# Row halves in turn for the first mixer's scores, and a new order of operations

## The chip, the cores and the metric

The kernel runs on one core of a Trainium2 chip. Its engines are TensorE (PE, with its weight loads as PEld), VectorE (DVE), ScalarE (ACT), GpSimd (POOL) and SyncE (SP), which issues most transfers. The metric is the device time of one execution in microseconds; less is better.

## The reference

A trunk of two layers over 256 tokens of 1024 channels, in fp32. Layer 0 mixes tokens with sliding-window attention with sinks, layer 1 with latent attention, and each mixer stands between two half-step SwiGLU feed-forwards with 2816 hidden channels:

```python
for i in range(DEPTH):
    x = x + 0.5 * swiglu(rmsnorm(x, ffn_norm1[i]), ffn1_wg[i], ffn1_wu[i], ffn1_wd[i])
    h = rmsnorm(x, mix_norm[i])
    if i % N_MIXERS == 0:
        x = x + sliding_window_attention(h, positions, rel_bias, a_w_in[j], ...)
    else:
        x = x + latent_attention(h, positions, b_w_in[j], ...)
    x = x + 0.5 * swiglu(rmsnorm(x, ffn_norm2[i]), ffn2_wg[i], ffn2_wu[i], ffn2_wd[i])
```

The first mixer has 16 query heads of 64 channels and two key and value heads, each for eight query heads:

```python
scores = jnp.einsum('bnqkgd,bnskd->bnkgqs', q, kb) * scale + bias
scores = jnp.where(valid, scores, NEG)
m = jnp.maximum(jnp.max(scores, axis=-1, keepdims=True), sink)
p = jnp.exp(scores - m)
denom = jnp.sum(p, axis=-1, keepdims=True) + jnp.exp(sink - m)
o = jnp.einsum('bnkgqs,bnskd->bnqkgd', p / denom, vb)
```

The scores' contraction thus runs over 64 channels, half of PE's 128 rows.

## The kernel before

The tokens are two tiles of 128 (t = 0 and 1). Every large weight comes in pieces of 128 x 1024 (`raw`); ACT casts a piece to a rounded high part (`whi`, line 402), and DVE subtracts to get the low part (`wlo`, line 397). A product then takes three matmuls: high by high, high by low, low by high (lines 735 to 737, 783 and 854).

Feed-forward: in chunks of 256 hidden channels, gate and up (line 854), then on DVE and ACT the gate function (lines 860 to 870), in which the product `h` is cast to a high part (line 656 on ACT, 660 on DVE) and a low part is subtracted (870), then down (783).

First mixer (`mixer_a`): per token tile, keys and values (KV), the queries in two halves of eight heads, norms, and transposes (line 688) of keys to `kTa` and of queries to `q`. In `q`, two heads lie above one another, the even one in partitions 0 to 63, the odd one in 64 to 127. Then for each key head g and parity par: the scores of four heads (line 1063), softmax (`softmax4`), transposes of p (688) and a copy to `pT`. When both parities are done, one operation multiplies by the values (line 1089, "PV"): the even heads write partitions 0 to 63 of the accumulator and the odd ones 64 to 127. The output projection (735 to 737, into `acc`) follows. For t = 0 four heads' scores of 128 columns fill one PSUM bank, for t = 1 (256 columns) two banks.

`softmax4` reads the scores with their bias out of PSUM on DVE (line 896, head by head, with the maximum), has exps and their sums on ACT (920), sums and reciprocal on DVE, and scales p in two portions (941 on DVE, 943 on ACT, 945 on POOL). PSUM has four banks named `w` for all of this, and an operation that needs a bank waits until the last reader of an earlier one has ended.

The order isn't the order of the code. Every operation is recorded with an engine (or several to choose from), an estimated cost and what it reads and writes. `Plan.run` then plays the program through by these costs: of the operations that are ready it takes the one that could start first, corrected by a table of penalties by the operation's name and engine (`PEN`), and within a stream of PE's operations it looks `WINDOW` places ahead; `SKEW` shifts the second tile's priority against the first's. Where an operation on PE that needs a new bank would start late, by over `FILLMIN`, the planner puts filler matmuls of 128 x 128 on the identity (line 1348) into that bank. It also has an idea of PE's clock (`pe_time`). The instructions are issued in the order that results, and the chip follows it engine by engine.

Two lines set which heads share a group before: `rows = slice(par * HD, (par + 1) * HD)`, one row half for all four, and `h = 8 * g + 2 * i + par`, so every second head.

## Time and profile before

| what | value |
|---|---|
| median of 3 runs (lowest to highest) | 953.3 us (952.58 to 954.87) |
| the profiled execution | 955.77 us, span 954.0 us |
| mean granted TensorE clock | 0.994 |
| PE busy | 940.6 us, 99% |
| DVE busy | 654.8 us, 69% |
| ACT busy | 490.4 us, 51% |
| POOL busy | 49.4 us, 5% |
| DMA | 160.07 MB, mean 168 GB/s |

The span goes from the first to the last instruction, and the execution's own time is a little longer. Busy PE includes the fillers, and matmuls are pipelined: a row's duration is longer than its distance from the next start. An fp32 matmul leaves two records in the trace, so 16 score matmuls are "x32", and one filler is two records; matmuls on the rounded parts leave one.

### The profile page before, as it was taken

To read this page: it belongs to the slowest core of one execution; us is meant where nothing else is said; L and a number is where in the kernel's file an instruction comes from. 1 tells how busy PE (TensorE), PEld (TensorE's weight loads), DVE (VectorE), ACT (ScalarE), POOL (GpSimd) and SP (SyncE) were. 2 spreads that over 40 slices of the span, in tenths; PEclk is the share of its full clock that TensorE was granted. 3 is DMA by queue.
4 is the path that set the end of the run, shared out by engine and by line. 5 is a ranking of instruction groups with operands and counts; after the bars stand their busy time and mean duration, and the time that the engine had idled before them with its cause. 6 is when DMAs were issued, how large, how long until landed. Compare 5 with 4: busy or idle time off the path is not lost.

```text
span 954.0 us, 16706 instructions
## 1 busy us (share of the span) xinstructions
PE 940.6 (99%) x6378; PEld 842.6 (88%) x6378; DVE 654.8 (69%) x1283; ACT 490.4 (51%) x854; POOL 49.4 (5%) x117
## 2 busy tenths in 40 slices
PE   8999999999999999999999999999999999999998
PEld 6999999988668999999989999998868889999997
DVE  6787777786767765666686656566698677565662
ACT  7484666355556543544464434443587445344540
POOL 2000000013000000000010000000431000000000
PEclk9999999999799999999999999999999999999999
DMA  8766556545115666565655656656201477556441
GB/s 287 232 209 209 167 176 192 165 133 179 43 45 178 219 200 199 166 200 165 201 172 173 204 178 187 203 162 199 95 1 46 141 238 225 192 177 209 159 140 45
DMA packets 119632, 160.07 MB, mean 168 GB/s; under 512 B 9264, under 2 KB 102912, under 8 KB 119552
## 3 DMA queue, kind: packets, MB, share of 16 engines
q1 hardware_dynamic: 119552, 159.00, 53.2%
q8 instruction: 50, 0.82, 0.4%
q14 instruction: 30, 0.25, 0.1%
HBM read 157.92 MB, written 1.05 MB: 167 GB/s over the span
## 4 chain that ended last, share of the span: by engine, by line
PE 93%; DVE 3%; DMA 2%; ACT 1%; issue 1%; SPq 0%; POOL 0%; DVEq 0%; ACTq 0%
PE w L854 47%; PE acc L783 26%; PE w L688 3%; PE acc L735 2%; PE acc L737 2%; PE acc L736 2%; PE w L735 1%; PE w L737 1%; PE w L736 1%; DMA raw<-in_ffn_wu_dram 1%; DVE wlo L397 1%; PE w L1262 1%; PE w L1209 1%; PE w L1063 1%; PE acc L1089 1%; PE acc L1274 1%
## 5 line engine op out<-in xcount | busy, mean ns | idle before, releaser
L854 PE MATMUL w<-xs,whi 128*128 128x256 f32 x2560 | 458.3, 282 | 0.0
L854 PEld LDWEIGHTS w<-xs,whi 128*128 128x128 f32 x2560 | 395.4, 189 | 3.4 <-ACT whi L402 0.2
L397 DVE TENSOR_TENSOR wlo<-raw,whi 128x1024 fp32r<-128x1024 f32 (+2 forms) x295 | 352.4, 1215 | 53.1 <-ACT whi L402 50.0
L402 ACT CAST whi<-raw 128x1024 fp32r<-128x1024 f32 (+2 forms) x295 | 303.8, 1042 | 121.1 <-PE acc L783 68.1
L854 PE MATMUL w<-xs,wlo 128*128 128x256 f32 x1280 | 360.5, 282 | 0.8 <-DVE wlo L397 0.8
L854 PEld LDWEIGHTS w<-xs,wlo 128*128 128x128 f32 x1280 | 241.0, 188 | 1.0 <-DVE wlo L397 1.0
L862 ACT ACTIVATE th<-h 128x256 f32<-128x256 f32 x80 | 33.5, 419 | 202.6 <-DVE h L860 202.6
L783 PE MATMUL acc<-wlo,pT 128*128 128x512 f32 x352 | 113.5, 396 | 0.0
L783 PE MATMUL acc<-whi,pT 128*128 128x512 f32 x352 | 113.5, 396 | 0.0
L783 PE MATMUL acc<-whi,t 128*128 128x512 f32 x352 | 113.3, 396 | 0.0
L860 DVE TENSOR_TENSOR h<-w,rb 128x256 f32<-128x256 f32 x80 | 34.0, 424 | 112.3 <-PE w L854 111.2
L783 PEld LDWEIGHTS acc<-whi,t 128*128 128x128 f32 x352 | 66.1, 188 | 16.3
L783 PEld LDWEIGHTS acc<-wlo,pT 128*128 128x128 f32 x352 | 66.1, 188 | 15.4
L783 PEld LDWEIGHTS acc<-whi,pT 128*128 128x128 f32 x352 | 63.4, 189 | 12.0
L870 DVE TENSOR_TENSOR t<-h,pT 128x256 fp32r<-128x256 f32 x80 | 34.0, 425 | 28.4 <-ACT pT L656 27.6
L864 DVE SCALAR_TENSOR_TENSOR th<-th,w 128x256 f32<-128x256 f32 x80 | 33.5, 419 | 26.5 <-ACT th L862 26.5
L656 ACT CAST pT<-h 128x256 fp32r<-128x256 f32 x61 | 24.8, 406 | 32.2 <-DVE h L866 32.0
L735 PE MATMUL acc<-whi,xs 128*128 128x512 f32 x96 | 39.9, 415 | 0.1
L737 PE MATMUL acc<-whi,xs 128*128 128x512 f32 x96 | 38.2, 398 | 0.4 <-DVE xs L674 0.4
L736 PE MATMUL acc<-wlo,xs 128*128 128x512 f32 x96 | 37.8, 394 | 0.0
L920 ACT ACTIVATE p<-p,st 128x128 f32<-128x128 f32 (+1 forms) x64 | 31.2, 491 | 10.2 <-DVE st L911 6.6
L735 PE MATMUL w<-whi,xs 128*128 128x512 f32 (+2 forms) x96 | 36.2, 377 | 0.0
(190 smaller groups left out, 814.6 us busy)
## 6 DMA issues: line engine op xcount, KB each, us to landing
raw<-in_ffn_wd_dram SPq DMA_DIRECT2D x88, 512.0 KB, 4.7
raw<-in_ffn_wg_dram SPq DMA_DIRECT2D x175, 256.0 KB, 3.9
raw<-in_ffn_wu_dram SPq DMA_DIRECT2D x175, 256.0 KB, 4.3
raw<-in_a_w_in_dram SPq DMA_DIRECT2D x10, 512.0 KB, 4.5
raw<-in_a_w_out_dram SPq DMA_DIRECT2D x8, 512.0 KB, 4.1
raw<-in_b_w_out_dram SPq DMA_DIRECT2D x8, 512.0 KB, 3.8
raw<-in_b_w_in_dram SPq DMA_DIRECT2D x4, 416.0 KB, 3.5
whi<-in_b_w_uq_dram SPq DMA_DIRECT2D x4, 384.0 KB, 3.1
```

Of the source, the lines that this page charges most:

```text
L397: V.tensor_tensor(out=lo[:, c], in0=raw[:, c], in1=hi.t.bitcast(F32)[:, c], op=ALU.subtract)
L402: op("ACT", c_act(m), lambda c=c: A.copy(out=hi[:, c], in_=raw[:, c]), [(raw, key_)], [(hi, key_)], seq="wh", pen=pen, prio=pr, name="W")
L735: T.matmul(o, lhsT=hi, rhs=wh, start=start, stop=False)
L736: T.matmul(o, lhsT=hi, rhs=wl, start=False, stop=False)
L737: T.matmul(o, lhsT=lo, rhs=wh, start=False, stop=stop)
L783: T.matmul(acc[nh].t, lhsT=a[:, ft, t0 : t0 + P], rhs=wt[:, nh * 512 : (nh + 1) * 512], start=(c == 0 and ft == 0 and i == 0), stop=(final ...
L854: T.matmul(o, lhsT=wt[:, sl], rhs=xs[:, p, :, kt], start=(kt == j == i == 0), stop=(kt == KT - 1 and j == 1 and i == 2))
L860: op("DVE", 0.345, lambda h=h, ps=ps: V.tensor_tensor(out=h.t, in0=ps[:, :FC], in1=rb.t, op=ALU.mult), [ps, rb], [h], name=nm)
L862: op("ACT", c_act(FC, 0.05), lambda th=th, h=h: A.activation(th.t, h.t, AF.Tanh, scale=0.5), [h], [th], name=nm)
L864: op("DVE", 0.345, lambda th=th, ps=ps: V.scalar_tensor_tensor(out=th.t, in0=th.t, scalar=1.0, in1=ps[:, :FC], op0=ALU.add, op1=ALU.mult), ...
L870: op("DVE", 0.36, lambda h=h, hthi=hthi, htlo=htlo, fb=fb: V.tensor_tensor(out=htlo[:, fb], in0=h.t, in1=hthi[:, fb].bitcast(F32), op=ALU. ...
L920: A.activation(pv(i), pv(i), AF.Exp, bias=nm[:, i : i + 1], scale=1.0 if scale is None else scale[:, i : i + 1], accum_out=den[:, i : i + 1],)
```

## The change

Four consecutive heads now form a group, so that within it even and odd heads alternate, one in each row half, into one bank for the even and one for the odd. Softmax is called on these two banks; for t = 0 both are read into one tile of p. The product with the values follows each group, on half of the accumulator's columns.

```diff
@@ mixer_a
-            o, pTs = buf(f"acc{t}", [P, 512]), []
-            for par in range(2):
-                name = f"S{t}.{g}{par}"
-                rows = slice(par * HD, (par + 1) * HD)
-                banks = [buf("w", [P, 512]) for _ in range(t + 1)]
-                for k, bk in enumerate(banks):
-                    def fn(k=k, bk=bk, rows=rows, g=g):
-                        for i in range(k * per, (k + 1) * per):
-                            T.matmul(
-                                bk[:, (i % per) * nk : (i % per + 1) * nk], lhsT=qT[rows, 4 * g + i, :],
-                                rhs=kT[rows, g, :nk], start=True, stop=True,
-                            )
-
-                    pe(t, 4, 512 * C_MM, fn, [(qT, g)] + [(kT, j) for j in range(t + 1)], [bk], name)
+            o = buf(f"acc{t}", [P, 512])
+            for hf in range(2):
+                name = f"S{t}.{g}{hf}"
+                banks = [buf("w", [P, 512]) for _ in range(2)]
+
+                def fn(banks=banks, g=g, hf=hf):
+                    for i in range(2):
+                        for par in range(2):
+                            rows = slice(par * HD, (par + 1) * HD)
+                            T.matmul(banks[par][:, i * nk : (i + 1) * nk], lhsT=qT[rows, 4 * g + 2 * hf + i, :],
+                                     rhs=kT[rows, g, :nk], start=True, stop=True)
+
+                pe(t, 4, nk * 2 * C_MM, fn, [(qT, g)] + [(kT, j) for j in range(t + 1)], banks, name)
...
-            def pvf(g=g, pTs=pTs, o=o):
-
-                for kt in range(t + 1):
-                    for par in range(2):
-                        T.matmul(o[par * HD : (par + 1) * HD, :], lhsT=sha["v", kt][:, g * HD : (g + 1) * HD],
-                                 rhs=pTs[par][kt].t, start=(kt == 0), stop=(kt == t))
+                def pvf(g=g, hf=hf, pT=pT, o=o):
+
+                    for kt in range(t + 1):
+                        for par in range(2):
+                            T.matmul(o[par * HD : (par + 1) * HD, hf * 256 : (hf + 1) * 256],
+                                     lhsT=sha["v", kt][:, g * HD : (g + 1) * HD],
+                                     rhs=pT[kt][:, par * 256 : (par + 1) * 256], start=(kt == 0), stop=(kt == t))
@@ the first weight's load
-                def load(j=j):
+                def load(j=j, q=nc.sync if len(wtiles) else nc.scalar):
@@ the planner's numbers (a few of them)
-WINDOW = 20
+WINDOW = 26
-SKEW = [1, 7, 8, 3, 4, 2]
+SKEW = [1, 7, 5, 7, 8, -5]
-    "S": {"ACT": 0.1, "PE": -0.2},
+    "S": {"ACT": 0.1, "PE": -0.05, "POOL": 0.15, "*": 0.05},
-POOLPEN = 1
-FILLMIN, FILLFROM = 0.5, 2.0
+POOLPEN = 0
+FILLMIN, FILLFROM = 0.35, 2.0
```

The table of penalties has new numbers in nearly every row, some costs are new, and the planner's idea of the clock has another threshold. So the order is new in the whole program. In numbers of instructions: fillers 34 before and 26 after, namely 8 and 9 at the start, 8 and 9 in the first mixer, 18 and 8 in the second. The casts of `h` (80 in the shared chunks) were 61 on ACT and 19 on DVE and are all on DVE. Of the 64 scalings of p, POOL had none and has 12.

PE in the first mixer's attention, before: line 1063 are the scores (`kTa` by `q`; 128 columns for the first token tile, 256 for the second), 688 the transposes of keys (`kna`) and of p, 1348 the fillers, 1089 PV.

```order
L688 MATMUL w<-ident,kna 128x128 x2
L1348 MATMUL w<-ident 128x128 x3
L1063 MATMUL w<-kTa,q_2869 128x128 x16
L688 MATMUL w<-ident,kna 128x128 x2
L1348 MATMUL w<-ident 128x128 x5
L1063 MATMUL w<-kTa,q_2938 128x256 x6
L688 MATMUL w<-ident,p 128x128 x8
L1063 MATMUL w<-kTa,q_2938 128x256 x2
L1089 MATMUL acc_3170<-pT,va_96 64x512 x2
L688 MATMUL w<-ident,p 128x128 x4
```

PE in the same place after, from the third group of the first tile on; lines 1080, 697, 1103 and 1363 are what 1063, 688, 1089 and 1348 were, `t` is the queries before their transposes, and 744 and 745 are projections.

```order
L1080 MATMUL w<-kTa,q_2804 128x128 x4
L697 MATMUL w<-ident,kna 128x128 x2
L1080 MATMUL w<-kTa,q_2804 128x128 x4
L697 MATMUL w<-ident,p 128x128 x8
L1103 MATMUL acc_3101<-pT,va_96 64x256 x2
L1080 MATMUL w<-kTa,q_3001 128x256 x4
L1103 MATMUL acc_3101<-pT,va_96 64x256 x2
L697 MATMUL w<-ident,t_3118 128x128 x4
L1080 MATMUL w<-kTa,q_3001 128x256 x4
L1363 MATMUL acc_3159<-ident 128x128
L744 MATMUL acc_3159<-whi,xs 128x512
L745 MATMUL acc_3159<-wlo,xs 128x512
```

The sixteen score matmuls of the first tile stood in one row and now stand in four groups of four; the first two of them are ahead of this piece, the first with 12 projections of 256 columns behind it, the second with 24 of 512 (six of them ahead of one set of transposes). The five fillers stand eleven rows below this piece.

DVE in the same place after: 909 are the reads of scores, 920 and 923 the maximum with the sink, 946 and 947 sum and reciprocal, 406 the low part of a weight, 1044 the scaling of the second tile's keys.

```order
L406 TENSOR_TENSOR wlo<-raw,whi 128x1024
L920 SCALAR_TENSOR_TENSOR st<-st,nsink 128x4
L923 TENSOR_TENSOR st<-sink,st 128x4
L406 TENSOR_TENSOR wlo<-raw,whi 128x1024
L946 TENSOR_TENSOR st<-st 128x4
L947 RECIPROCAL st<-st 128x4
L406 TENSOR_TENSOR wlo<-raw,whi 128x1024
L946 TENSOR_TENSOR st<-st 128x4
L947 RECIPROCAL st<-st 128x4
L909 ISA p,st<-w,S_849 128x128
L909 ISA st 128x1
```

And before, at the end of the first tile's scores, with the lines 896, 906, 909, 932 and 933 for the same operations:

```order
L1030 TENSOR_SCALAR kTa<-w,ka 128x2x128
L906 SCALAR_TENSOR_TENSOR st<-st,nsink 128x4
L909 TENSOR_TENSOR st<-sink,st 128x4
L896 ISA p,st<-w,S_1336 128x128
L896 ISA st 128x1
L896 ISA p,st<-w,S_1336 128x128
L896 ISA st 128x1
```

No low part of a weight stood between these reads; now three stand ahead of the third group's. Between the first and the last read of the first mixer's scores there were three of them and are seven.

PE at the end of the second mixer's attention, before: 1260 and 1262 are its scores for the second tile, 1274 its product with the values.

```order
L1262 MATMUL w<-S_8142 128x128
L1274 MATMUL acc_8351<-pT,q_7779 64x128 x4
L1348 MATMUL w<-ident 128x128 x13
L688 MATMUL w<-ident,p 128x128 x8
L735 MATMUL acc_8455<-whi,xs 128x512
```

And after, with 1275, 1277 and 1289 for these:

```order
L1363 MATMUL w<-ident 128x128 x3
L1275 MATMUL w<-S_7860,S_8316 128x128
L1277 MATMUL w<-S_8316 128x128
L1275 MATMUL w<-S_7860,S_8316 128x128
L1277 MATMUL w<-S_8316 128x128
L1275 MATMUL w<-S_7860,S_8316 128x128
L1277 MATMUL w<-S_8316 128x128
L1275 MATMUL w<-S_7860,S_8316 128x128
L1277 MATMUL w<-S_8316 128x128
L1363 MATMUL w<-ident 128x128 x2
L697 MATMUL w<-ident,p 128x128 x8
L744 MATMUL acc_8455<-whi,xs 128x512
```

Before, sixteen score matmuls (two groups of heads) stood ahead of this piece without a break, and six projections between its transposes of p and the next ones. Now eight stand together and the group before them earlier, and 24 projections lie between the two sets of transposes.

## Rows read from the trace of the kernel before

**Rows 1.** The page: busy time of PE, and the chain's share by engine.
```profile
PE 940.6 (99%) x6378; PEld 842.6 (88%) x6378; DVE 654.8 (69%) x1283; ACT 490.4 (51%) x854; POOL 49.4 (5%) x117
...
PE 93%; DVE 3%; DMA 2%; ACT 1%; issue 1%; SPq 0%; POOL 0%; DVEq 0%; ACTq 0%
```

**Rows 2.** Stretches: from:to, length, busy us (x instructions) by engine, granted clock, DMA.
```profile
0.00:11.45 11.45, 7.64 (x36) 6.10 (x37) 5.37 (x16) 7.06 (x16) 3.89 (x20) 1.00 0.75 234
...
236.60:249.25 12.65, 10.48 (x80) 8.30 (x80) 11.52 (x73) 8.67 (x40) 0.70 (x1) 1.00 0.14 43
249.25:259.49 10.24, 10.24 (x28) 6.05 (x26) 6.67 (x29) 3.82 (x13) 0.00 (x0) 0.50 0.16 51
...
670.00:735.20 65.20, 63.13 (x419) 50.00 (x418) 53.05 (x210) 47.20 (x141) 22.72 (x40) 1.00 0.12 37
```

**Rows 3.** PE in order of time at the start: start, duration, what, [idle before].
```profile
8.91 0.50 PE L736 MATMUL w<-wlo,xs 128*128 128x512 f32 x1 [0.94 <-DVE wlo L397]
...
10.46 1.25 PE L688 MATMUL w<-ident,x 128*128 128x128 f32 x8 [0.83 <-DMA x<-in_x_dram]
```

**Rows 4.** PE in order of time, first mixer.
```profile
236.83 0.83 PE L1348 MATMUL w<-ident 128*128 128x128 f32 x6
237.69 2.88 PE L1063 MATMUL w<-kTa,q 64*128 64x128 f32 x32
...
241.04 1.38 PE L1348 MATMUL w<-ident 128*128 128x128 f32 x10
242.82 2.10 PE L1063 MATMUL w<-kTa,q 64*128 64x256 f32 x12 [0.40 <-DVE kTa L1030]
244.85 0.72 PE L688 MATMUL w<-ident,p 128*128 128x128 f32 x4
247.22 0.63 PE L688 MATMUL w<-ident,p 128*128 128x128 f32 x4 [1.64 <-DVE st L932]
...
251.42 3.77 PE L1063 MATMUL w<-kTa,q 64*128 64x256 f32 x8
...
262.63 0.60 PE L688 MATMUL w<-ident,p 128*128 128x128 f32 x4
262.99 0.48 PE L735 MATMUL acc<-whi,xs 128*128 128x512 f32 x1
...
267.25 1.13 PE L1063 MATMUL w<-kTa,q 64*128 64x256 f32 x4
268.31 0.50 PE L735 MATMUL acc<-whi,xs 128*128 128x512 f32 x1
268.64 0.39 PE L736 MATMUL acc<-wlo,xs 128*128 128x512 f32 x1
268.87 0.40 PE L737 MATMUL acc<-whi,xs 128*128 128x512 f32 x1
```

**Rows 5.** PE in order of time, end of the second mixer's attention.
```profile
731.41 3.17 PE L1348 MATMUL w<-ident 128*128 128x128 f32 x26
734.41 1.04 PE L688 MATMUL w<-ident,p 128*128 128x128 f32 x8
```

**Rows 6.** DVE's groups by form, 236.5 to 285 us: count | busy us, mean ns | idle before.
```profile
L896 DVE CUSTOM_DVE_ANT_0 p<-w,S 128x256 f32<-128x256 f32 x16 | 6.0, 415 | 0.0
L397 DVE TENSOR_TENSOR wlo<-raw,whi 128x1024 fp32r<-128x1024 f32 x4 | 4.9, 1216 | 0.0
L896 DVE CUSTOM_DVE_ANT_0 p<-w,S 128x128 f32<-128x128 f32 x16 | 3.6, 285 | 0.0
```

**Rows 7.** ACT's groups by form in the same stretch.
```profile
L920 ACT ACTIVATE p<-p,st 128x128 f32<-128x128 f32 x16 | 6.2, 387 | 2.6 <-DVE st L906 2.6
```

**Rows 8.** The feed-forward: a stretch inside it, and the casts of h over the whole span.
```profile
350.00:650.00 300.00, 300.00 (x2073) 278.22 (x2072) 195.84 (x290) 137.97 (x180) 2.71 (x10) 1.00 0.61 185
...
L656 ACT CAST pT<-h 128x256 fp32r<-128x256 f32 x61 | 24.8, 406 | 32.2 <-DVE h L866 32.0
L660 DVE CAST pT<-h 128x256 fp32r<-128x256 f32 x19 | 5.6, 295 | 0.7
```

## Prediction before the run

> **What bounds the kernel now.** I read the page's busy times and chain first [rows 1]. TensorE (PE) is busy for 940.6 of 954.0 us and holds 93% of the chain, so a gain must come out of PE's own time: fewer or faster matmuls, fewer idle stretches, or less time at the low clock. Busy doesn't mean useful, though. The planner puts filler matmuls (line 1348) where it expects PE to wait, a filler counts as busy, and so does a matmul at half clock. So I went on to the stretches [rows 2] and to PE in order of time [rows 3 to 5]. In both feed-forward pairs around the mixers PE has no gap at all at the full clock, as in 350 to 650 us [rows 8]; there is nothing to win there. What can be won lies in four places.
>
> First, the first mixer's attention, 236.6 to 268 us. The scores of all sixteen heads of the first token tile start together at 237.69, and from then on PE waits for sixteen heads of softmax: 0.83 and 1.38 us of fillers, idle times of 0.40 and 1.64 us [rows 4], while VectorE (DVE) is busy for 11.52 of 12.65 us [rows 2]. Second, right behind the 1.64 us comes a stretch of 10.24 us in which the granted clock is 0.50, the lower of the two levels (1.2 GHz) [rows 2]: 5.1 us lost. Third, the end of the second mixer's attention: 26 filler records (13 fillers) run for 3.17 us before the transposes of p at 734.41 [rows 5]. Fourth, the first 11.45 us, where PE is busy for 7.64 us and waits 0.94 us for a weight's low part and 0.83 us for x [rows 2, 3].
>
> The profiled execution took 955.77 us (span 954.0), 2.5 us over the median of 953.3. I make the sum against 955.8 and scale the result by 953.3/955.8.
>
> **Scores in both row halves.** A score matmul has 64 rows of contraction. Before, all those of one parity, thus one row half, stand in a row. Eight records of one half alone take 3.77 us at the half clock, 0.47 each, so 0.236 at the full clock [rows 4]. But the twelve records at 242.82, eight of one half and then four of the other, take 2.10 us, not 12 x 0.236 = 2.83 [rows 4]: the four of the other half have run beside the first eight. So the row halves do overlap, and the after-order, which alternates them and gives each half its own bank, can pair all records. Before, the six runs take 2.88 + 2.10 + 1.13 + 3.77/2 + 1.13 + 1.13 = 10.3 us at the full clock (the 1.13 of 267.25 is a row; the two others of its kind are like it) [rows 4]. After, four runs of 256 columns take 4 x 0.236 = 0.94 each and four of 128 columns half of that, together 5.7, and with 0.15 us of entry and tail for each of eight groups 6.9. That is -3.4 us of PE time; bounds: -4.6 (perfect pairs) and 0 (no more overlap than now).
>
> What is it worth when DVE has to read the scores out? DVE's reads take 3.6/16 = 0.23 us a head in the first tile and 6.0/16 = 0.38 in the second [rows 6], so 0.9 and 1.5 us for four heads, against 0.6 and 1.1 us in which PE will make them. PE is then ahead of its reader, where before it was about level. The Trainium skill, page "TensorEngine Tiling (Array Packing)", section "PSUM Bottleneck", says just that: tiling speeds up the matmuls and not the evacuation of PSUM, which may become the bound. By it the -3.4 would be 0. It is a rival below. I keep -3.4, because more other work stands between the scores than before: between the first and last score matmul 36 projections of 512 columns and 12 of 256, where there were 24 of 512.
>
> **Price of more runs.** The score runs grow from six to seven and those of PV from four to seven, so there are eight more passages between 64-wide and 128-wide matmuls. After a run of scores the first projection takes 0.50 instead of 0.39 us; after a run of full 128 x 128 transposes (ahead of 262.99) it takes 0.48 [rows 4]. The passage from 64 rows thus costs no more than any other, some 0.1 us. The same page, section "Key Properties", has it that changing the tiling mode drains the engine; the row shows at most 0.02 us for it. Eight passages at 0.1 would be 0.8, but half of them replace other passages: +0.4, bounds 0 and 0.8.
>
> **Order of the first mixer.** The scores of the first tile now come in four portions with projections between them, so softmax starts earlier behind other work. PE gives up there what it has now, 0.83 + 1.38 us of fillers and 0.40 + 1.64 us idle, 4.2 us. What comes instead? The order has nine fillers there (before eight); five took 1.38 us [rows 4], so nine some 2.5. Then DVE: it has 7 casts of a weight's low part between its first and last read of scores, where it had 3, each 1.22 us [rows 6]. Three of them stand before the reads that free the banks of the first tile's last group: three casts 3.7, four reads 0.9, the two reads waited for 0.5, and about ten small operations that I estimate at 1.4, make 6.5 us, against 18 projections x 0.23 us [rows 4] + transposes and scores (some 1.4) = 5.5 us on PE. So PE waits some 1.0 us there, then about as much again, in pieces, for the second tile's keys and the transposes behind them. Before the five fillers, the softmax of the third group needs four exps of 0.39 us and sums behind two casts [rows 6, 7]; I take 1.0 us beyond the fillers. Smaller waits for PV's operands 1.2. Together 6.7 us: +2.5 against now; bounds -1.7 (fillers alone) and +7.4 (all four added casts, 4.9 us, exposed as well).
>
> **The half clock.** In the trace it fell after a stretch that held a 1.64 us idle time, single-half scores and short transposes [rows 4], and nowhere else between the start and the output. The waits that I expect are shorter and lie apart, with projections between them; the scores fill both halves. I take it as gone: -5.1, with 0 as the other bound.
>
> **Second mixer.** Before, the scores of the second tile's last two groups stand together, and both softmaxes are waited for with PE empty: 13 fillers, 3.17 us [rows 5]. After, those groups stand apart, with five fillers around the last one, and 24 projections instead of 6 lie between the two sets of transposes of p. 13 fillers fewer 5 are worth 8 x 3.17/13 = 2.0 us. DVE, 53.05 of 65.2 us busy there [rows 2], also loses 12 scalings of p to ScalarE (ACT) and GpSimd. -2.0, bounds -3.2 and +1 (the waits that fillers no longer show come back as idle).
>
> **Start.** The first weight's four loads go to ACT's queue, beside those of x on SP's. The two waits of 0.94 and 0.83 us [rows 3] can shrink, but four more issues stand before ACT's table load and squares, and x now shares the transfers: -0.4, bounds -1.5 and +0.8.
>
> **Moved at no cost.** In the feed-forward all 80 casts of h go to DVE, where 61 were on ACT: 0.295 instead of 0.406 us each [rows 8]. That adds 18 us to DVE over some 700 us in which it is idle for a third (195.84 of 300 us busy [rows 8]) and PE has no gap; it also saves a change of engine in the chain. 0; if DVE were late there, PE would stop at the next chunk for one cast, 0.3 us.
>
> **Sum:** -3.4 + 0.4 + 2.5 - 5.1 - 2.0 - 0.4 = -8.0, so 947.8 for such an execution, and 945 as a median.
>
> **Rivals.** (1) The low clock comes back: DVE's casts make PE wait over 1.5 us in one piece, as at 245.6, and PE runs at 0.50 for another 10 us. For it speaks that the waits I expect are of about that size; against it, that the order puts fillers and projections between. 945 + 5.1 less some 0.5 us of waits that lie inside = 949.6. (2) DVE is the limit of the attention, and the faster scores only wait longer for their reader: 945 + 3.4 = 948.4. The 91% busy DVE of 236.6 to 249.25 [rows 2] speaks for it, the added projections against. (3) The row halves don't pair up, so the change doesn't do what it says: also 948.4. The twelve records speak against it. (4) Slower: DVE's order in the first mixer. All four added casts are exposed (4.9 us) and the low clock comes back twice (10.2 us): 945 + 15.1 = 960. It becomes slower than before once waits and low clock together give back more than 8 us, so one recurrence alone isn't enough; DVE would have to hold PE for over 3 us besides.
>
> **How the numbers follow.** Forecast 0.53 (941 to 948), (1) 0.23, (2) 0.12, (3) 0.04, (4) 0.08. A measurement of this kernel can tell about 0.3%, 2.9 us, from no change. Faster (under 950.4): nearly all of the forecast, 0.6 of (1), 0.7 of (2) and (3): 0.52 + 0.14 + 0.11 = 0.77. Slower (over 956.2): most of (4), 0.07. The rest, 0.16, within. The range reaches from the forecast's better bound, 940, to the upper part of (1), 952.
>
> **What would show it.** Right: score runs of 128 columns of about 0.6 us and of 256 columns of about 1.1 for four heads, records in pairs; no stretch at the clock 0.50 between 230 and 270 us; the filler run at the second mixer's end at 0.7 us or less. Wrong: PE idle behind the casts of line 397 for over 1.5 us in one piece, the clock at 0.50 in the first mixer, or a gap on PE in the feed-forward waiting for the cast of h.

## The result and the profile after

| | before | after |
|---|---|---|
| median (lowest to highest) | 952.94 us (952.19 to 954.87) | 939.66 us (939.45 to 942.47) |
| ratio, 95% interval | | 0.9864 [0.9841, 0.9888] |
| the profiled execution | 955.77 us, span 954.0 | 939.52 us, span 937.7 |
| mean granted clock | 0.994 | 1.0 |

Faster by 13.3 us, more than forecast and 0.3 us beyond the better end of the range. Of the changed kernel the page's busy times and chain, for [rows 1]:

```profile
PE 929.8 (99%) x6386; PEld 837.4 (89%) x6386; DVE 664.9 (71%) x1303; ACT 478.9 (51%) x822; POOL 56.0 (6%) x129
...
PE 95%; ACT 2%; DMA 1%; DVE 0%; issue 0%; SPq 0%; POOL 0%; ACTq 0%
```

PE still holds the chain, and is busy for 10.8 us less. Stretches of the changed kernel, for [rows 2, 8] (columns as there): the start, the first mixer's attention, a stretch of the feed-forward, the second mixer's attention.

```profile
0.00:11.05 11.05, 8.01 (x38) 6.81 (x39) 4.87 (x16) 6.87 (x16) 3.89 (x20) 1.00 0.84 279
228.30:258.00 29.70, 29.08 (x198) 21.97 (x198) 26.92 (x107) 24.51 (x79) 7.42 (x8) 1.00 0.40 127
350.00:650.00 300.00, 300.00 (x2093) 279.20 (x2092) 199.32 (x303) 131.35 (x164) 2.71 (x10) 1.00 0.58 184
660.00:720.00 60.00, 59.67 (x400) 47.76 (x399) 49.11 (x199) 48.49 (x140) 24.39 (x44) 1.00 0.16 52
```

The granted clock is 1.00 in all of these stretches; the one at 0.50 is gone from the profiled execution (by its mean clock of 0.998, another execution of the four, 942.47 us, still has some). DVE is busy for 91% of the first mixer's attention, the share that it had before in the 12.65 us of [rows 2]. PE in order of time, first mixer of the changed kernel, for [rows 4] (1080 scores, 1363 fillers, 697 transposes):

```profile
228.27 0.71 PE L1080 MATMUL w<-kTa,q 64*128 64x128 f32 x8
...
230.97 1.20 PE L1080 MATMUL w<-kTa,q 64*128 64x128 f32 x8
...
238.25 0.71 PE L1080 MATMUL w<-kTa,q 64*128 64x128 f32 x8
238.90 0.44 PE L697 MATMUL w<-ident,kna 128*128 128x128 f32 x2
239.26 1.01 PE L1080 MATMUL w<-kTa,q 64*128 64x128 f32 x8
240.20 0.66 PE L697 MATMUL w<-ident,p 128*128 128x128 f32 x4
241.07 0.63 PE L697 MATMUL w<-ident,p 128*128 128x128 f32 x4 [0.21 <-DVE st L909]
...
242.21 1.13 PE L1080 MATMUL w<-kTa,q 64*128 64x256 f32 x8
...
248.59 1.28 PE L1363 MATMUL w<-ident 128*128 128x128 f32 x10
...
253.11 0.33 PE L697 MATMUL w<-ident,p 128*128 128x128 f32 x1 [0.40 <-POOL p L959]
...
255.04 2.00 PE L1080 MATMUL w<-kTa,q 64*128 64x256 f32 x16
```

Four heads of 256 columns take 1.13 us in 8 records; before, two heads in 4 records took that [rows 4]. The row halves run side by side. The two idle times of 0.21 and 0.40 us are all there is of idle on PE here. The end of the second mixer's attention, for [rows 5]:

```profile
712.31 0.63 PE L697 MATMUL w<-ident,p 128*128 128x128 f32 x4 [0.33 <-ACT pT L665]
...
715.54 0.94 PE L1363 MATMUL w<-ident 128*128 128x128 f32 x6
...
718.10 0.61 PE L1363 MATMUL w<-ident 128*128 128x128 f32 x4
718.55 1.04 PE L697 MATMUL w<-ident,p 128*128 128x128 f32 x8
```

To place the difference I cut both traces at the same gate and up matmuls (the 960th, 1201st, 2880th and 3301st record of that line). A mixer's stage takes in some feed-forward on either side, and the last stage ends with PE's last matmul:

| stage, us | start and first feed-forward | first mixer | two middle feed-forwards | second mixer | last feed-forward |
|---|---|---|---|---|---|
| before | 193.85 | 152.52 | 313.30 | 187.25 | 103.31 |
| after | 193.61 | 142.22 | 313.41 | 181.43 | 103.31 |
| difference | -0.24 | -10.30 | +0.11 | -5.82 | 0.00 |

The sum, -16.25 us, is the difference of the two profiled executions. The medians differ by 13.3, since the profiled execution of before was 2.5 us over its median. Within the first mixer's stage PE's time divides up as follows (from each record's start to the next start, without idle; "filled" is the kernel before with six more fillers, below, "old groups" the new planner's numbers with the groups of before, and "new groups" the reverse; a wait that shows no gap between records counts as time of the kind that waited):

| us | scores | PV | transposes of p | fillers | idle | stage |
|---|---|---|---|---|---|---|
| before | 11.72 | 6.64 | 6.49 | 2.22 | 3.50 | 152.52 |
| before, filled | 9.94 | 5.76 | 5.51 | 3.72 | 1.87 | 147.22 |
| after | 7.41 | 6.24 | 5.82 | 2.12 | 0.62 | 142.22 |
| after, old groups | 10.31 | 5.76 | 5.18 | 1.06 | 0.01 | 141.89 |
| before, new groups | 8.19 | 6.44 | 5.68 | 5.30 | 1.94 | 147.08 |

### The profile page after: what moved, and what is told of

Its sections match the earlier page's. It is cut to its first block, busy times and chain, and to the rows that moved or that the text cites. A ratio compares the mean times of both kernels' runs of the same rounds, so it can differ in the third digit from the quotient of the medians.

```text
span 937.7 us, 16805 instructions
## 1 busy us (share of the span) xinstructions
PE 929.8 (99%) x6386; PEld 837.4 (89%) x6386; DVE 664.9 (71%) x1303; ACT 478.9 (51%) x822; POOL 56.0 (6%) x129
## 4 chain that ended last, share of the span: by engine, by line
PE 95%; ACT 2%; DMA 1%; DVE 0%; issue 0%; SPq 0%; POOL 0%; ACTq 0%
PE w L863 48%; PE acc L792 26%; PE w L697 3%; PE acc L744 2%; PE acc L746 2%; PE acc L745 2%; PE w L744 2%; PE w L746 2%; PE w L745 2%; PE w L1224 1%; ACT p L934 1%; PE acc L1195 1%; PE w L1080 1%; PE w L632 1%; PE acc L1103 1%; PE w L1363 1%
## 5 line engine op out<-in xcount | busy, mean ns | idle before, releaser
L736 POOL TENSOR_TENSOR var<-ss 128x1 f32<-128x1 f32 x12 | 2.4, 201 | 590.4 <-ACT junk L709 590.4
L726 DVE SCALAR_TENSOR_TENSOR xs<-w,gcols,xs 128x128 fp32r<-128x128 f32 x96 | 28.8, 345 | 10.7 <-ACT xs L667 9.0
```

Of the source, the lines that this page charges most:

```text
L726: V.scalar_tensor_tensor(out=xv(1, t)[:, kt], in0=b[:, (kt % 4) * P : (kt % 4 + 1) * P], scalar=gc[:, gi * KT + kt : gi * KT + kt + 1], in ...
```

## The experiments

**Pairing, alternation, the low clock, fillers.** My first theory was the prediction's: paired scores and a missing low clock make the difference. One kernel puts all scores on one row half (the odd heads get the even heads' scores):

```diff
-                            rows = slice(par * HD, (par + 1) * HD)
+                            rows = slice(0, HD)
```

> The changed kernel, except that all score matmuls of the first mixer read the lower row half (partitions 0 to 63), so that the scores of the odd heads are those of their even neighbours: that part of the computation is left out. Number, size, banks and order of all instructions stay, and no two score matmuls can run side by side. If the pairing of the row halves counts on the path, PE's score runs grow from 7.4 us in all to about 10 and the kernel is slower by 2.5 to 3.4 us (942 to 943). If DVE's reading of the scores is the limit, the time stays at 939.7 within 0.5. If the single half also brings the low clock back, a stretch at 0.50 shows in the first mixer and it is 947 or more.

944.66 us (943.77 to 945.72), ratio 0.9900 [0.9867, 0.9934], 1.7 us over what I expected; first mixer's stage 146.19, +3.97; clock 1.0.

```profile
228.48 1.16 PE L1080 MATMUL w<-kTa,q 64*128 64x128 f32 x8
...
257.49 3.72 PE L1080 MATMUL w<-kTa,q 64*128 64x256 f32 x16
```

1.16 us instead of 0.71, and 3.72 instead of 2.00 for 16 records of 256 columns: two halves nearly double the rate. This seemed to settle that the new groups pay. It doesn't: this kernel's scores take 12.09 us of PE, more than those of the old groups (10.31), for a reason that comes below. It does show that PE has little to spare either: of 4.7 us more of scores 4.0 show.

The next one keeps the groups and issues one half after the other:

```diff
-                    for i in range(2):
-                        for par in range(2):
+                    for par in range(2):
+                        for i in range(2):
```

> The changed kernel with the four score matmuls of a group in another order: the two of one row half, then the two of the other, into the same two banks. If PE pairs only neighbours that alternate, about half of the pairing is lost: 1 to 2 us slower. If it looks ahead, as the run of twelve records before suggested, the records pair as now and the time stays at 939.7 within 0.5.

941.26 us (939.34 to 942.3), ratio 0.9857 [0.9819, 0.9894]; stage 142.33. The median is 1.6 us over the changed kernel's, as if half of the pairing were lost, but the mixer's stage didn't grow: in the profile the start's did (196.27 us, with PE idle for 1.6 us more). PE overlaps a run on one half with the run on the other behind it; turn by turn isn't needed, two halves close together are enough.

The kernel before with six fillers ahead of the transposes that PE waited 1.64 us for [rows 4]:

```diff
+            if o.name == "PT0.01" and e == "PE":
...
+                for _ in range(6):
+                    self.filler(ahead)
```

> The kernel before with six more filler matmuls ahead of the transposes of p that PE waited 1.64 us for, written into the accumulator that the next product with the values uses; the order of everything else is the same. If the idle time is what lets the clock fall, the stretch of 10 us at 0.50 is gone and the kernel takes 948 to 949 (5.1 us less, minus a little for fillers that end late). If the clock falls for another reason (the single-half scores or the short transposes), the stretch stays and the time stays at 953 or is up to 0.5 longer.

952.44 us (951.39 to 954.2), ratio 0.9978 [0.9957, 1.0]. Its PE and its stretch at the place of [rows 2]:

```profile
246.35 1.50 PE L1360 MATMUL acc<-ident 128*128 128x128 f32 x12
248.16 0.63 PE L700 MATMUL w<-ident,p 128*128 128x128 f32 x4 [0.30 <-DVE st L944]
...
249.25:259.49 10.24, 10.24 (x48) 6.34 (x47) 9.69 (x36) 6.48 (x24) 0.00 (x0) 1.00 0.16 51
```

With 0.30 us idle in place of 1.64 the clock stays at 1.00 and the stage is 5.3 us shorter. But the median is only some 2 us under before's (1.5 by the two medians, 2.1 by the ratio). The mean granted clock is known of every execution. Of the seventeen of before beside this kernel, eight are at 1.00 and take 951.03 to 952.5 us, two at 0.998, and seven at 0.990 to 0.995, which take 957.3 to 960.87. Of this kernel's twelve none is under 0.997. So the fillers took the long stretch at the low clock away, and that stretch comes in some executions of before, not in all.

The changed kernel without any filler:

```diff
-            self.filler(bank)
```

> The changed kernel without its 26 filler matmuls; all else in the same order. If the fillers only cover waits and keep the clock up, then without them PE idles where they stood (some 4 us in the mixers in pieces of up to 1.3 us) and the time either stays at 939.7 within 1, with the clock at 1.00 throughout, or a stretch at 0.50 comes into a mixer and costs up to 5 us. If fillers are in the way (they end after what they wait for), it gains up to 2 us.

940.73 us (939.27 to 941.9), ratio 0.9858 [0.982, 0.9895]; mixers' stages 141.99 and 180.81. The clock was low once, in the first feed-forward behind 1.66 us idle for a small load:

```profile
41.36 0.36 PE L556 MATMUL w<-rel,h 32*128 32x16 f32 x2 [1.66 <-DMA h<-in_c_steps_dram]
...
41.98:45.39 3.41, 3.41 (x18) 3.41 (x17) 3.24 (x13) 0.53 (x1) 0.00 (x0) 0.50 0.80 252
```

**Groups or numbers.** The change has two halves, which can be had apart: the groups (scores, softmax, PV) and the planner's numbers with the order that follows, to which I count the queue of the first weight's loads. The planner makes its order anew in either kernel.

```diff
@@ groups alone, on before
-                banks = [buf("w", [P, 512]) for _ in range(t + 1)]
+                banks = [buf("w", [P, 512]) for _ in range(2)]
...
+                    for i in range(2):
+                        for par in range(2):
+                            rows = slice(par * HD, (par + 1) * HD)
@@ numbers alone, on after: the same lines the other way round
```

> The kernel before with the new groups of four heads (both row halves, two banks) alone; the planner's numbers, its second mixer and its start are the old ones. Theory: the pairing of row halves is worth some 4 us wherever it stands, and the second mixer's gain comes from the planner's numbers. Then the first mixer's stage (152.5 us before with the low clock, 147.2 without) comes to 143 us, the second mixer's stays at 187 to 188 us against 181.4 in the changed kernel, and the median is some 948 to 949. Rival: the pairing pays only in the new order, because DVE reads the scores too late in the old one: first mixer's stage 146 to 147, median 951 to 953.

951.62 us (950.33 to 955.28), ratio 0.9984 [0.9966, 1.0003]; first mixer's stage 147.08, second's 187.77. My theory had expected 143 and a median of 948 to 949. Against before without its low clock (147.22) the groups gave 0.1 us. PE:

```profile
241.65 0.90 PE L1071 MATMUL w<-kTa,q 64*128 64x128 f32 x10
242.94 0.71 PE L1071 MATMUL w<-kTa,q 64*128 64x128 f32 x6 [0.38 <-DVE st L900]
243.94 3.26 PE L1071 MATMUL w<-kTa,q 64*128 64x128 f32 x24
247.44 0.94 PE L1354 MATMUL w<-ident 128*128 128x128 f32 x6 [0.24 <-DVE st L900]
...
249.77 0.66 PE L688 MATMUL w<-ident,p 128*128 128x128 f32 x4 [0.95 <-ACT pT L656]
```

24 records take 3.26 us where the changed kernel's rate would be 2.1 (0.71 for 8): each group waits until DVE has read banks of those before. What is saved on scores (1.75 us) comes back as fillers (1.58) and a longer PV (0.68).

> The changed kernel with the old groups (four heads of one row half), the planner's new numbers kept. Theory: the numbers alone give the second mixer's gain (stage 181.4 us) and some of the first mixer's waits, not the pairing: first mixer's stage 145 to 147 us, median 943 to 945. Rival: the numbers were only good for the new groups: first mixer's stage 148 us and more, or the low clock again, median over 946.

939.49 us (938.93 to 940.72), ratio 0.9851 [0.982, 0.9882]; stages 141.89 and 181.41. **The whole gain without the new groups.** My theory had expected 943 to 945. PE shows why the old groups are no slower:

```profile
228.18 1.71 PE L1072 MATMUL w<-kTa,q 64*128 64x128 f32 x16
...
238.22 1.71 PE L1072 MATMUL w<-kTa,q 64*128 64x128 f32 x16
239.86 0.66 PE L697 MATMUL w<-ident,p 128*128 128x128 f32 x4
...
240.57 1.06 PE L1357 MATMUL w<-ident 128*128 128x128 f32 x8
...
244.30 2.00 PE L1072 MATMUL w<-kTa,q 64*128 64x256 f32 x12
```

16 records in 1.71 us are two groups, one of each half, that stand together in this order and so overlap (one half alone would need 2 x 1.16, halves in turn 2 x 0.71). The rest of the scores' 2.9 us (10.31 against 7.41) is balanced in the table: PV 0.48 and transposes of p 0.64 us shorter, fillers 1.06 and idle 0.61.

**The second mixer.**

```diff
@@ on after: SKEW, PENW and PEN of before in the second mixer alone
-            pen += PEN.get(cls, {}).get(eng if isinstance(eng, str) else "*", 0.0)
+            pen += (OLDPEN if self.phase == 4 else PEN).get(cls, {}).get(eng if isinstance(eng, str) else "*", 0.0)
@@ apart from that, on after: every scaling of p of the second mixer on DVE
-                    if e == "DVE":
+                    if e == "DVE" or name[:2] == "SB":
```

> The changed kernel, with the old skew and penalties in the second mixer only (thresholds, costs and window stay new). Theory: the gain of some 6 us in the second mixer comes from its own penalties and skew: its stage goes back to 185 to 188 us, median 943.5 to 946.5. Rival: it comes from the planner's common numbers (costs, threshold of fillers, window): stage 181 to 183, median 939.5 to 941.

945.7 us (944.75 to 946.08), ratio 0.9913 [0.9882, 0.9943]; stage 186.52, +5.09, with 4.76 us of fillers instead of 2.03 and 2.02 idle instead of 0.33. The second mixer's gain is its own order, 5.1 of 5.8 us.

> The changed kernel, order unchanged, but each scaling of p in the second mixer that stands on ACT or POOL is done by DVE. Theory: DVE limits the second mixer's attention, and taking work from it gave a good part of the gain: stage 183 to 185.5 us instead of 181.4, median 941.5 to 944. Rival: the gain is in PE's own work and order (fewer fillers, less idle), with DVE beside it: stage 181.4 to 182, median 939.5 to 940.5.

941.13 us (940.04 to 941.49), ratio 0.9864 [0.9827, 0.9901]; stage 182.32, +0.89. Even with all scalings on DVE most of the gain stays; taking work from it is the lesser part.

**Who limits the first mixer?** The seven low-part casts between the first and last read of scores were made twice, in the changed kernel and in the one with old groups (there with 12 for 16, as fewer operations read the scores); DVE then has fourteen of them in both:

```diff
+                    for _ in range(2 if 0 < len(reading) < 16 else 1):
```

> The changed kernel, order unchanged, with each of the seven low-part casts that stand on DVE between the first and the last read of the first mixer's scores made twice: 7 x 1.22 = 8.5 us more for DVE. Theory: DVE limits this stretch in the changed kernel (29.1 of 29.7 us busy for PE beside it), so faster scores only wait longer: most of the 8.5 us shows, the first mixer's stage goes from 142.2 to 148 us or more. Rival: DVE has slack there, and the shorter scores were eaten by PE's own added passages: stage 144 us or less.

949.7 us (947.87 to 950.01), ratio 0.9938 [0.9911, 0.9966]; stage 150.07, +7.85.

```profile
239.79 0.48 PE L1085 MATMUL w<-kTa,q 64*128 64x128 f32 x2
243.46 1.17 PE L1085 MATMUL w<-kTa,q 64*128 64x128 f32 x6 [3.19 <-DVE st L914]
...
238.00:248.00 10.00, 6.81 (x40) 4.81 (x40) 8.93 (x30) 5.96 (x17) 4.10 (x3) 0.83 0.53 157
```

> The same seven casts made twice in the kernel with the new numbers and the old groups (its first mixer's stage was 141.9 us). If both kernels stand against the same limit, DVE, the stage grows as in the changed kernel (148 us or more in both, within 1 us of one another). If the old groups are bound by PE and the new by DVE, it grows by at least 2 us less than there.

949.6 us (948.18 to 951.32), ratio 0.9939 [0.9911, 0.9968]; stage 151.75, +9.86. I had expected the two to grow alike within 1 us; they differ by 2.0. Both kernels stand against DVE: of 8.5 us nearly all shows. Some of it may be the clock, which was at 0.50 for 6.8 us in the first profile (behind idle times of 3.19 and 1.52 us) and for 10.2 in the second (behind 1.51). But the second kernel's two executions at a mean clock of 1.00 took 949.05 and 949.55 us and its four at 0.995 948.18 to 951.32, so there the low clock isn't what made it longer. Three doubled casts ahead of the third group's reads (3.66 us) made PE wait 3.19 us at the fourth group, so DVE had 0.5 us to spare there.

**Fillers again, and small loads.** The kernel with old groups, fillers at the start only, and then the table of steps loaded at 22 us:

```diff
-            self.filler(bank)
+            if a < 100:
+                self.filler(bank)
@@ and then
+        if i == 1:
+            nc.sync.dma_start(out=steps0, in_=c_steps)
```

> New numbers, old groups, and no filler after the start (the order else the same): without fillers the mixers' stages were 0.2 and 0.6 us shorter in the changed kernel. Expected: stages 141.6 and 180.8, median 0.5 to 1.0 us under the kernel with fillers (939.5), so 938.5 to 939. If waits make the clock fall, a stage grows by 2 us or more.

939.47 us (938.46 to 940.54), ratio 0.9829 [0.9803, 0.9855]; stages 141.87 and 180.79. The fillers in the mixers are worth no more than 0.6 us either way, and nothing in the median (939.49 with them).

> The kernel without fillers once more, with the 16 KB table of steps loaded at about 22 us into a place of its own, not at 35 us. In the profiles so far PE waited from 0 to 1.9 us for it at 40 us, a different time in each execution, and in two of them the clock was low behind it. Theory: this wait makes the spread of the first stage (193.5 to 197.7 us): stage 193.2 to 193.6, no wait at 40 us, median 0.3 to 1.5 us under the other one of this call and its runs closer together. Rival: the wait only moves to the next late transfer: stage and median as in the other one.

939.7 us (938.71 to 942.04), ratio 0.9836 [0.9809, 0.9864]: no gain. PE waits at the same matmul, by the times for its other operand: `rel` was still loaded at 35.38 us and took 4.9 us to land. The trace names another releaser:

```profile
40.42 0.36 PE L558 MATMUL w<-rel,steps 32*128 32x16 f32 x2 [0.38 <-PE w L864]
```

So both went early, now in the changed kernel, beside the changed kernel itself:

```diff
+            nc.sync.dma_start(out=rel0, in_=rel_bias)
+            nc.sync.dma_start(out=steps0, in_=c_steps)
```

> The changed kernel with two small loads, the bias table (2 KB) and the table of steps (16 KB), issued at about 22 us and not at 35 us; the order on PE, DVE and ACT is the same. The run with the steps alone still waited 0.4 us at 40 us, for the bias table then. Theory: this wait makes the spread of the first stage (193.5 to 197.7 us in the profiles): no wait at 40 us, stage 193.0 to 193.6, median 0.2 to 1.5 us under the changed kernel in this call and its runs closer together. Rival: the start's spread comes from the first 12 us or from other transfers: stage and spread as in the changed kernel.

**930.05 us (929.7 to 930.73), ratio 0.9742 [0.9707, 0.9777].**

> The changed kernel once more, as the other side of the run with both early loads on the same chip. Expected: 939.7 to 941 us, first mixer's stage 142.2, second mixer's 181.4, first stage anywhere from 193.5 to 197.

940.24 us (939.8 to 940.62), ratio 0.985 [0.9818, 0.9882]. Ten microseconds, and hardly from the wait: the middle feed-forwards' stage is 305.57 instead of 313.41. Gate and up matmuls there, by form, 380 to 600 us, of the changed kernel and then of the one with both loads early (count | busy, mean ns):

```profile
L863 PE MATMUL w<-xs,whi 128*128 128x256 f32 x768 | 137.2, 282 | 0.0
...
L863 PE MATMUL w<-xs,whi 128*128 128x256 f32 x783 | 134.5, 277 | 0.0
```

From start to start they follow each other every 113.7 ns in the mean instead of 118.4. The two new tiles (512 and 64 bytes of each partition) had moved all rotating tiles in the on-chip memory by 576 bytes, those of weights among them: by the program's addresses `whi` begins at byte 75136 of a partition, a multiple of 128, and before at 74560, off by 64. Four kernels took this apart:

```diff
@@ on after (16 columns: 64 bytes; 32: 128 bytes), and on before (16)
+    cp.tile([P, 16], F32, name="pad")
@@ both loads early, weights off by 64 again
+    cp.tile([P, 112], F32, name="pad")
```

> The changed kernel with 64 bytes per partition left unused ahead of the rotating tiles, nothing else. With both small loads early, the gate and up matmuls of the two middle feed-forwards had a pitch of 113.5 ns where they had 118, and the tiles of weights stood 64 bytes later modulo 128 (whi at 75136 = 587 x 128, where it was at 74560 = 582.5 x 128). Theory: the place of the weights gave that, not the loads: stage of the two middle feed-forwards 305.6 us (313.4 in the changed kernel), median 930.5 to 932. Rival: the loads gave it: stage 313.4, median 939.5 to 941.

934.02 us (931.68 to 935.98), ratio 0.9796 [0.9769, 0.9823]; middle stage 305.57. An unused tile of 64 bytes, and no load moved: the place did it. Which of the moved tiles counts, the weights or others, no run shows.

> The changed kernel with 128 bytes per partition unused at the same place: the weights are as far off a multiple of 128 bytes as in the changed kernel. If a multiple of 128 matters: stage of the two middle feed-forwards 313.4 us, median 939.5 to 941. If any shift helps (or another multiple): 306 to 310 us.

944.7 us (944.25 to 944.89), ratio 0.9904 [0.989, 0.9919]; middle stage 314.55. I had expected the changed kernel's 939.5 to 941; the matmuls follow each other every 119.1 ns in all four feed-forwards, so 128 bytes aren't the same as none.

> The kernel before with the 64 unused bytes. If the place of the weights acts by itself, the two middle feed-forwards' stage goes from 313.3 to 305.5 us here too and the median from 953.7 to some 944 to 946; then the change and the place add up. If it only acts with the new order: 951 to 955.

949.54 us (947.89 to 950.13), ratio 0.9953 [0.9936, 0.997]; middle stage 309.20, last one 100.71. Of the last three feed-forwards the second and third run at 113.7 ns here (stages -4.10 and -2.60), with the changed kernel's order the first and second.

> Both small loads early as before, with more unused bytes, so that the weights are off a multiple of 128 bytes as in the changed kernel (whi at 75584 = 590.5 x 128). It shows the loads alone: no wait at 40 us, stage of the two middle feed-forwards 313.4, first stage 193.5 to 194.2 (192.4 in the shifted one, of which some 1.5 us came from the matmuls' pitch), median 0.2 to 1.0 us under the changed kernel (940.2), so 939.2 to 940.

939.97 us (939.11 to 940.07), ratio 0.9854 [0.9839, 0.9868]; middle stage 313.41, first stage 194.09. PE doesn't wait at 40 us any more, but the first stage lies between those of the changed kernel's two profiles (193.61 and 194.71). Another wait was longer, the one for x near 5 us (1.44 us against 1.27 and 1.20); the rest isn't accounted for.

## Why the prediction was right and wrong

The measured 939.66 us lies 0.3 us under the better end of the range. Two terms carried it there, the waits of the first mixer and the second mixer; the term of the scores failed too, but the other way.

**Right:** that it becomes faster; that PE has the chain and the feed-forwards give nothing (+0.11 us, 80 casts of `h` moved at no cost); that the low clock goes (in the profile); and that the halves pair up (0.71 and 1.13 us where 0.6 and 1.1 were named, though two of the four runs of 128 columns took 1.20 and 1.01). The start's -0.24 for -0.4 decides nothing, since this stage varies from 192.4 to 197.7 us between the profiles.

**Scores, -3.4: near in size on PE, wrong in worth.** From the filled before, PE's score time went from 9.94 to 7.41 us, -2.5. But the groups alone are worth 0.1 us in the old order, and in the new order the old groups are 0.3 us quicker. The failed step is "I keep -3.4, because more other work stands between the scores". In the new order, of the 2.9 us that the groups save on scores, 1.7 come back as fillers and idle time and 1.1 as PV and transposes of p. Rival (2) named the mechanism of the larger part, and the doubled casts show it: DVE, with 0.5 us to spare at the first tile's last group, sets when scores are read. The Trainium skill, page "TensorEngine Tiling (Array Packing)", section "PSUM Bottleneck", says that tiling speeds up TensorE but not the evacuation of PSUM. The runs agree: stage 147.22 and 147.08 us without and with the groups. The rival's time, 948.4, was still wrong, since other terms were.

**More runs, +0.4:** between the two kernels in the new order PV and transposes of p cost 1.1 us more with the groups. The sign was right, the size too small: over the bound of 0.8. How much of it is the passages and how much are waits isn't shown; without fillers the transposes alone take 6.92 us instead of 5.82.

**Waits of the first mixer, +2.5: the wrong sign.** I counted waits of 4.2 us before and 6.7 after. Over the stage, fillers and idle were 5.72 us before and 2.74 after, -3.0, under my bound of -1.7. Of the 1.5 us that I hadn't counted before, 1.2 stood behind the attention and are gone:

```profile
284.80 0.50 PE L737 MATMUL acc<-whi,xs 128*128 128x512 f32 x1 [0.45 <-DVE xs L674]
...
308.12 0.39 PE L854 MATMUL w<-xs,wlo 128*128 128x256 f32 x1 [0.76 <-DVE wlo L397]
```

The step that failed is the sum of what comes instead, 6.7 us: its fillers were right (2.5 forecast, 2.12 measured), its waits were not (4.2 and 0.62, beside some 0.8 inside two of the score runs). The largest of them was the race at the first tile's last group, DVE's 6.5 us against PE's 5.5. In the changed kernel's DVE, the third of the three casts and the first read behind them:

```profile
237.29 1.20 DVE L406 TENSOR_TENSOR wlo<-raw,whi 128x1024 fp32r<-128x1024 f32 x1
...
239.00 0.29 DVE L909 CUSTOM_DVE_ANT_0 p<-w,S 128x128 f32<-128x128 f32 x1
```

The third group's scores begin at 238.25 and the read at 239.00, nearly on time for the fourth group, whose 1.01 us instead of 0.71 hold all that PE waited. The casts lie where PE had 24 projections to do. Beside the last 18 of them and what follows, 233.95 to 239.26 us, DVE needed 5.6 us (233.93 to 239.49) and not 6.5, since two of the four reads that I had counted were done by then. I had priced DVE's added work as exposed; but the first tile's scores now spread over 12 us (228.27 to 240.27) where they stood in 2.88, and PE has its projections in between, not fillers. That the groups have nothing to do with it, the old groups in this order show (fillers and idle 1.07 us).

**Half clock, -5.1: right for the profiled execution, too much for the median.** Without the idle time the stage is 5.3 us shorter, but the median fell by about 2, as only seven of seventeen executions of before were at 0.995 or less. I scaled one execution by 953.3/955.8, as if its low clock were in the median too.

**Second mixer, -2.0: right sign, a third of the size.** It gave 5.82 us, beyond the bound of -3.2. The step that failed is the count: I took only the thirteen fillers at the end, which came to 0.94 + 0.61 us for 3.17. By kinds, fillers fell from 4.26 to 2.03 us, idle from 2.32 to 0.33, transposes of p by 0.5. The idle times in the middle of the stage had stood in the trace before all along; I had not listed them:

```profile
700.10 0.66 PE L688 MATMUL w<-ident,p 128*128 128x128 f32 x4 [0.51 <-ACT S L658]
...
714.20 0.61 PE L688 MATMUL w<-ident,t 128*96 128x128 f32 x4 [0.44 <-DVE t L1231]
...
725.35 0.61 PE L688 MATMUL w<-ident,t 128*96 128x128 f32 x4 [0.69 <-ACT pT L656]
```

**The sum:** against the profiled execution the terms missed by -4.7 in the first mixer, -3.8 in the second and +0.3 elsewhere, which the low clock's part in the median brought back by some 3.

## A faster version

The kernel with both small loads early and the rotating tiles 576 bytes further on is the fastest, 930.05 us against 940.24 for the changed kernel beside it. Its 10 us are the place of these tiles above all (7.84 in the middle stage and, by the matmuls' pitch, 1.8 in the first). Against the unused 64 bytes alone it has 4 us less in the median; how much of that is the loads and how much the start's own variation isn't settled, as the loads alone gave nothing that can be measured.

## What to carry to other kernels

A change that brings a new structure and a new order should be taken apart by building each half: here the order gave everything and the structure nothing (which of the planner's numbers gave it wasn't taken apart), and a test that spoils the structure (one row half) pointed the other way. For a reordered stage, list all of its idle time and fillers before, not the largest place, and price an engine's added work only where the other engine arrives earlier than it. Look at a low clock in several executions before it goes into a median.

## What was not expected of the hardware

- Matmuls of 64 rows on the two row halves overlap also when all of one half are issued first: 142.33 against 142.22 us of stage, and 16 records of two groups in 1.71 us.
- The clock of 0.50 shows behind idle times of 1.5 to 1.9 us, at more than one place: 249.25 to 259.49 us behind 1.64 us, 41.98 to 45.39 behind 1.66 us. The same wait of 1.64 us had 10.24 us at 0.50 behind it in the kernel before and 3.41 in the one with 64 unused bytes. By their mean clock, eight of seventeen executions of before had none; whether PE waited less in them isn't known.
- Where the rotating tiles begin changed the pitch of matmuls of 256 columns between 118 or 119 and 113.7 ns, 7.8 us over two feed-forwards. Shifts of 64 and of 576 bytes gave it, one of 128 didn't. A multiple of 128 isn't the rule: in the changed kernel no shift and one of 1024 bytes (both loads early, unshifted) gave the same 118.4 ns, and 128 gave 119.1. With 64 bytes one of the last three feed-forwards stays at 119 ns, the third in the changed kernel and the first in the kernel before. What decides there is open.
